# First feed-forward layer of a diffusion backbone: 14 of 22 hidden tiles as seven half-size products, in three segments with a written order

## The chip, the cores and the metric

One core of one Trainium2 chip runs the whole program. The metric is device time in microseconds (us). The engines are TensorE (matrix products; PE in the rows), VectorE (DVE), ScalarE (ACT), GpSimd (POOL) and SyncE (SP, which here only issues loads).

## The reference

Two layers over 512 latent tokens of width 1024. Layer 0 mixes tokens by latent attention with 256 context tokens and by a Fourier transform, layer 1 by two kinds of convolution. Each layer ends with the same channel mixer, a SwiGLU feed-forward of hidden width 2816 behind a modulated norm:

```python
sh1, sc1, g1, sh2, sc2, g2 = ada_mod(c, ada_w[i], ada_b[i])
...
x = x + g1 * mix
x = x + g2 * swiglu(modulate(rms_norm(x, norm2_g[i]), sh2, sc2), ffn_w1[i], ffn_w3[i], ffn_w2[i])
...
def swiglu(h, w1, w3, w2):
    return (jax.nn.silu(h @ w1) * (h @ w3)) @ w2
```

`ada_mod` turns the conditioning vector into six modulation vectors for each layer, 48 columns of 128 values.

## The kernel before

Everything is kept transposed: channels on the 128 partitions, the 512 tokens along the free axis. Each fp32 operand is split into a high part (rounded to fp32r) and a low part (the rest), and each product is three matmuls: high x high, high x low, low x high (`mm3`, L115). A weight unit (128 x 1024) is loaded by SP into a `wraw` buffer (three), its high part is cast on ScalarE and its low part is subtracted on VectorE (`split`, L95); five pairs `whi`/`wlo` hold the results.

**The plain form (layer 0, `ffn`, L996).** The hidden width is 22 tiles of 128, f = 0 to 21. For each, `proj` (L962) multiplies the norm's output by a w1 unit and a w3 unit: 8 steps over the channels x 3 matmuls x 512 tokens, twice, 48 matmuls. The first five units are done in two halves of the tokens, since the norm of the second half of the tokens is made meanwhile. Three of these five (the "head units", `HU`) lie in the large slots 14, 13 and 8. `done` puts Silu on the w1 result (ScalarE), multiplies it by the w3 result (VectorE, L1008) and splits the product into high and low. All 22 stay resident, then each of the 8 output tiles takes 22 x 3 matmuls of w2, and `residual` (L271) adds the result to `X`. The last output tile is done in two halves of 256 tokens, so that the statistics (`s1`) and the norm (`s2`, `s3`) of the next layer can start between.

**The block form (layer 1, `ffn_blocks`, L1046).** Here the first NPL = 3 tiles are plain and each further one is a 2 x 2 block product: rows are w1 and w3, inner halves are the channels 0 to 511 and 512 to 1023, columns are the tokens 0 to 255 and 256 to 511. Seven products of half size replace eight (Strassen's method in Winograd's form): 7 x 4 channel steps x 3 = 84 matmuls of 256 tokens (`prod`, L1188). It needs sums of the operands:
- of the norm's output, once: `forms` (L1084), four additions or subtractions of 128 x 1024 and four splits, from full copies of the norm's output that `Norm` then writes as well;
- of the weights, per tile: `load_sums` (L1113) has SP load one quarter twice into a tile and POOL add two other quarters by an accumulating transfer (L1120), then `prep_block` (L1122) makes two more sums on VectorE and splits them all. `load_raw` (L1107) loads the three quarters that are used as they are.

`block_window` (L1198) writes one tile's seven products together with the preparation of the next tile (`prep`) and the epilogue of the tile before (`tail`). The hidden tiles come in three segments of 8, 7 and 7 (`SEGS`); behind each, its part of the output product is added to `X`, so that only one segment's results need be kept.

**What sets the order.** In general the framework's scheduler orders the instructions of each engine by its own estimates and may hoist loads far ahead. From the end of `proj` in `ffn_blocks` the order is the written one (`manual_schedule`, L1262).

**Modulation columns.** Each column is a load of 128 x 1024 (512 KB) into one of two `ada` buffers and one VectorE reduction (L154), for some columns a ScalarE pass on 128 values. 56 columns, those that the end of layer 0 and layer 1 need, wait in a list `bg`; `pump(2)` (L178) runs two behind each hidden tile and output tile of layer 0.

Of the kernel before, what the change touches and what calls it, by code (L numbers as in the profile page):

```python
# [9 lines left out]
F32 = mybir.dt.float32  # L10
# [7 lines left out]
P = 128  # L18
# [15 lines left out]
FH = (5, 14)  # L34
# [27 lines left out]
def tile_dit(  # L62
# [100 lines left out]

    def ada_jobs(l, key, base, n, pin=True):
        m = const.tile([P, n], F32, name=f"m_{l}_{key}")
        mods[l, key] = m
        return [lambda j=j: ada_tile(m[:, j:j + 1], l * 48 + base + j, ada[l * 48 + base + j], scb, pin=pin)
                for j in range(n)]
# [9 lines left out]
    def pump(n):  # L178
        for _ in range(min(n, len(bg))):
            bg.pop(0)()  # L180

# [743 lines left out]
    n2_0 = Norm("n2_0", mods[0, "s2"])  # L925
# [6 lines left out]
    def ffn_srcs(l):  # L932
        return [w[l, f] for f in range(NPL if l in BLK else FF) for w in (w1, w3)]

# [61 lines left out]
    def ffn(l, nrm, head, sq_next=None, make_next=None):  # L996
        gt = {}
        held = {}

        def done(i, p):  # L1000
            f = i // 2
            if i % 2 == 0:
                s = t2k()
                A.activation(s, p, AF.Silu)
                held[f] = s
                return
            g = t2k()
            V.tensor_mul(g, p, held.pop(f))  # L1008
            if f in (4, 5):
                gt[f] = slot(("6a", "6b")[f % 2], [P, 2, S], F32R)  # L1010
            elif f % 2 == 0:
                d = slot(4 + f // 2, [P, 2, 2, S], F32R)
                gt[f], gt[f + 1] = d[:, 0], d[:, 1]
            split(gt[f][:, 0, :], gt[f][:, 1, :], g)
            pump(2)

        proj(ffn_srcs(l), nrm, done, NF, head=head)
        g2 = mods[l, "g2"]
        for mt in range(KT):
            chunks = [unit(w2[l, mt, :, a:a + n, :], n * P) for a, n in W2CHUNKS]  # L1020
            p = ps()
            nxt = None
            if mt == KT - 1 and make_next is not None:
                pump(len(bg))
                nxt = make_next()
            for hf, (a, b) in enumerate(((0, S),) if mt < KT - 1 else HALF):
                for ci, ((wh, wl), (k0, n)) in enumerate(zip(chunks, W2CHUNKS)):
# [528 lines left out]
```

## Time and profile before

| what | value |
|---|---|
| median of 3 runs | 1190.65 us (1190.1 to 1190.69) |
| profiled execution | 1190.21 us, span of the instructions 1188.3 us |
| TensorE / VectorE / ScalarE / POOL busy | 99% / 67% / 40% / 11% of the span |
| mean granted TensorE clock | 0.998 |
| feed-forward of layer 0 | about 297 to 662 us after the span's start |
| feed-forward of layer 1 | about 834 to 1185 us |
| read from memory | 174 MB |

Times in rows are us from the span's start. A row of the timeline gives start, duration, engine, line, operation, tiles written and read, and in brackets how long the engine had been idle before it and what ended that. Matmul durations overlap: the distance from one start to the next is what a matmul costs.

### The profile page before, as it was taken

How to read it: one execution, taken by the hardware profiler on the slowest of the kernel's cores; microseconds unless marked ns; L12 is line 12 of the kernel's file. 1: busy time of each engine (PE TensorE's matmuls, PEld its weight loads, DVE VectorE, ACT ScalarE, POOL GpSimd, SP SyncE). 2: the span in 40 equal slices, each digit the busy share in tenths (PEclk: the TensorE clock that was granted, in tenths of full speed). 3: DMA queues.
4: the chain of work that ended last, by engine and by line, in shares of the span. 5: the costliest groups of instructions: out<-in, count | busy, mean ns of one | idle time of the engine just before them, and what ended most of it. 6: DMA issues, size and time to landing. Idle time of an engine off the chain costs nothing.

```text
span 1188.3 us, 16786 instructions
## 1 busy us (share of the span) xinstructions
PE 1174.4 (99%) x6627; PEld 993.1 (84%) x6627; DVE 802.1 (67%) x1302; ACT 478.8 (40%) x787; POOL 127.6 (11%) x110
## 2 busy tenths in 40 slices
PE   8999999999999999999999999999999999999998
PEld 6777856669988888888888988888999899989997
DVE  7979876756665655554443699976887468757852
ACT  5545455544432323232222564334654235424530
POOL 1012300000000000000002496200000000000000
PEclk9999999999999999999999999999999999999999
DMA  9872033374266556655555133222168247816432
GB/s 340 300 286 109 1 106 93 120 248 144 67 216 209 181 189 200 197 182 188 167 162 168 54 106 107 72 89 90 49 181 221 91 109 185 219 54 162 107 110 86
DMA packets 52226, 177.24 MB, mean 149 GB/s; under 512 B 5682, under 2 KB 6578, under 8 KB 51891
## 3 DMA queue, kind: packets, MB, share of 16 engines
q1 hardware_dynamic: 49410, 166.21, 42.4%
q0 software_dynamic: 2736, 9.96, 4.9%
q8 instruction: 52, 0.85, 0.3%
q14 instruction: 28, 0.22, 0.1%
HBM read 174.05 MB, written 2.10 MB: 148 GB/s over the span
## 4 chain that ended last, share of the span: by engine, by line
PE 94%; DVE 3%; DMA 2%; ACT 1%; issue 0%; POOL 0%; ACTq 0%; DVEq 0%; SPq 0%
PE ps L116 21%; PE ps L117 21%; PE ps L118 21%; PE ps L1193 16%; PE ps L866 2%; PE ps L708 1%; PE ps L581 1%; PE ps L851 1%; PE ps L852 1%; PE ps L853 1%; PE ps L871 1%; DVE t L211 1%; DMA s<-in_w 1%; PE ps L822 1%; PE ps L197 1%; PE ps L293 1%
## 5 line engine op out<-in xcount | busy, mean ns | idle before, releaser
L116 PE MATMUL ps<-s,whi 128*128 128x512 f32 (+1 forms) x1067 | 394.9, 370 | 1.2 <-DVE x L272 1.2
L117 PE MATMUL ps<-s,whi 128*128 128x512 f32 (+1 forms) x1067 | 391.2, 367 | 2.1 <-DVE s L217 2.1
L118 PE MATMUL ps<-s,wlo 128*128 128x512 f32 (+1 forms) x1067 | 390.8, 366 | 0.2 <-DVE wlo L97 0.2
L96 ACT CAST whi<-wraw 128x1024 fp32r<-128x1024 f32 (+2 forms) x127 | 129.7, 1024 | 281.0 <-PE ps L117 138.5
L116 PEld LDWEIGHTS ps<-s,whi 128*128 128x128 f32 x1067 | 201.8, 189 | 36.1 <-DVE x L272 1.6
L117 PEld LDWEIGHTS ps<-s,whi 128*128 128x128 f32 x1067 | 201.8, 189 | 35.4 <-DVE s L217 2.3
L118 PEld LDWEIGHTS ps<-s,wlo 128*128 128x128 f32 x1067 | 201.8, 189 | 34.4 <-DVE wlo L97 0.7
L97 DVE TENSOR_TENSOR wlo<-wraw,whi 128x1024 fp32r<-128x1024 f32 (+2 forms) x107 | 127.1, 1188 | 79.8 <-ACT whi L96 76.3
L1193 PE MATMUL ps<-s,whi 128*128 128x256 f32 x912 | 165.2, 283 | 0.1
L1193 PEld LDWEIGHTS ps<-s,whi 128*128 128x128 f32 x912 | 142.4, 192 | 0.6 <-DVE t L1217 0.3
L1193 PE MATMUL ps<-s,wlo 128*128 128x256 f32 x456 | 129.0, 283 | 0.0
L272 DVE SCALAR_TENSOR_TENSOR x<-ps,m_g,x 128x512 f32<-128x512 f32 (+1 forms) x67 | 43.9, 662 | 105.9 <-PE ps L118 105.9
L154 DVE CUSTOM_DVE_ANT_0 ada<-ada,scb,vec 128x1024 f32<-128x1024 f32 x80 | 100.2, 1279 | 0.5 <-DMA ada<-in_ada 0.5
L1193 PEld LDWEIGHTS ps<-s,wlo 128*128 128x128 f32 x456 | 87.5, 192 | 0.0
L1120 POOL DMA_DIRECT2D s<-in_w x19 | 16.8, 884 | 585.9 <-DMA s<-in_w 443.7
L1008 DVE TENSOR_TENSOR t<-ps,t 128x512 f32<-128x512 f32 x22 | 15.2, 692 | 71.3 <-PE ps L118 71.3
L96 ACT CAST whi<-s 128x1024 fp32r<-128x1024 f32 x38 | 39.7, 1047 | 54.0 <-PE ps L1193 28.1
L1369 DVE SCALAR_TENSOR_TENSOR ps<-s,vec,ps 128x512 f32<-128x512 f32 x78 | 55.8, 751 | 1.4 <-ACT ps L1366 0.9
L97 POOL TENSOR_TENSOR wlo<-wraw,whi 128x1024 fp32r<-128x1024 f32 x20 | 48.8, 2444 | 30.9 <-ACT whi L96 27.0
L117 PE MATMUL ps<-s,s 128*128 128x256 f32 (+1 forms) x160 | 50.2, 315 | 0.0
L118 PE MATMUL ps<-s,s 128*128 128x256 f32 (+1 forms) x160 | 50.1, 314 | 0.0
L116 PE MATMUL ps<-s,s 128*128 128x256 f32 (+1 forms) x160 | 48.3, 317 | 0.2 <-ACT s L216 0.2
(278 smaller groups left out, 1662.2 us busy)
## 6 DMA issues: line engine op xcount, KB each, us to landing
ada<-in_ada SPq DMA_DIRECT2D x82, 512.0 KB, 4.4
wraw<-in_w SPq DMA_DIRECT2D x74, 512.0 KB, 3.6
s<-in_w SPq DMA_DIRECT2D x19, 768.0 KB, 5.7
wraw<-in_w_in SPq DMA_DIRECT2D x20, 512.0 KB, 3.3
s<-in_w SPq DMA_DIRECT2D x38, 256.0 KB, 4.0
s<-in_w POOLq DMA_DIRECT2D x19, 512.0 KB, 5.5
s<-in_ada SPq DMA_DIRECT2D x16, 512.0 KB, 7.1
wraw<-in_w_out SPq DMA_DIRECT2D x16, 512.0 KB, 3.4
```

What stands on the lines that cost most here:

```text
L96: A.copy(hi, src)
L97: (eng or V).tensor_sub(lo, src, f32(hi))
L116: T.matmul(o, wh, ah, start=start, stop=False)
L117: T.matmul(o, wh, al, start=False, stop=False)
L118: T.matmul(o, wl, ah, start=False, stop=stop)
L154: i = V.tensor_tensor_reduce(raw, raw, scv, 1.0, vc("ada_b", idx), ALU.mult, ALU.add, accum_out=dst)
L272: V.scalar_tensor_tensor(X[m][:, a:b], psum, gcol, X[m][:, a:b], ALU.mult, ALU.add)
L866: T.matmul(p[64 * x:64 * x + 64, :], vh[t][:, 2 * j + x, :], ost["p", 2 * j + x, tp][:, s * S:(s + 1) * S], start=(t == 0), stop=(t == 5))
L1008: V.tensor_mul(g, p, held.pop(f))
L1120: G.dma_start(s13, w[:, :D], accum_op=ALU.add)
L1193: T.matmul(o, w, b, start=start and kk == 0 and i == 0, stop=kk == 3 and i == 2, skip_group_check=True)
L1369: V.scalar_tensor_tensor(dst, cp[:, w:w + S], vec[:, o + w:o + w + 1], src, ALU.mult, ALU.add)
```

## The change

Layer 0's feed-forward also runs through `ffn_blocks`, which is made to take plain and block tiles in one sequence; `ffn` is deleted. Tiles 0 to 2 stay in `proj`. Of the other 19, fourteen are blocks (`BLK[0]`) and 5, 10, 13, 17 and 20 are plain (`plain_window`: the 48 matmuls with the same places for `prep` and `tail`). Every plain tile has block tiles as neighbours. The norm before layer 0's feed-forward writes full copies into slots 5 and 7. The sums of weights lie in the two halves of slot 8 in layer 0 and are loaded two blocks ahead (`SB`), not three. The output product has three segments here too, in written order; in the last segment the last three output tiles (`TS`) are left to the scheduler, first their left halves, then their right halves, with statistics and norm of layer 1 between. The modulation columns have fixed places: 4 behind tiles 0 and 1, then two in a window that does not lead from a block to a block of the same segment (13 of 19 windows), then two behind each of the first two output tiles of a segment and one behind each of the others. Each reduction is followed on SP by the load of the column two further on, into the buffer that the reduction frees.

```diff
-FH = (5, 14)
...
-W2CHUNKS = ((0, 8), (8, 8), (16, 6))
 SEGS = ((0, 8), (8, 7), (15, 7))
 NPL = 3
+NA = 2
 UB = 5
-BLK = {1: tuple(range(NPL, FF))}
+BLK = {0: (3, 4, 6, 7, 8, 9, 11, 12, 14, 15, 16, 18, 19, 21), 1: tuple(range(NPL, FF))}
...
+        def load(self):
+            self.raw = units.tile([P, D], F32, tag="ada", bufs=AB, name=nm("ada"))
+            nc.sync.dma_start(self.raw, ada[self.idx])
+        def reduce(self):
+            V.tensor_tensor_reduce(self.raw, self.raw, scb, 1.0, vc("ada_b", self.idx), ALU.mult, ALU.add, accum_out=self.dst)
...
+    def pump_ahead(n):
+        for _ in range(min(n, len(bg))):
+            while gains:
+                gains.pop(0)()
+            job = bg.pop(0)
+            job.reduce()
+            gains.append(job.gain)
+            if len(bg) >= AB:
+                bg[AB - 1].load()
...
-    n2_0 = Norm("n2_0", mods[0, "s2"])
+    n2_0 = Norm("n2_0", mods[0, "s2"], (5, 7))
...
-    def ffn(l, nrm, head, sq_next=None, make_next=None):
...
+            if l == 0:
+                if "s8" not in st:
+                    st["s8"] = slot(8, [P, 2, D])
+                return st["s8"][:, i % 2, :]
...
+            if f < NPL - 1:
+                pump(2)
...
+        SB = 3 if l else 2
...
+        def prep_tile(f):
+            if f in blk:
+                return prep_block(f)
+            wf[f] = []
+            return prep_two(wf[f], (w1[l, f], w3[l, f]), D)
...
+            pump_ahead(na - na // 2)
...
+        def plain_window(f, tail, prep, after, na):
+            hh, hl = nrm.h
+            pss = [ps(), ps()]
+            s, g = t2k(), t2k()
+            def mms(i):
+                wh, wl = wf[f][i]
+                for k in range(KT):
+                    c = slice(k * P, (k + 1) * P)
+                    mm3(pss[i], wh[:, c], wl[:, c], hh(k), hl(k), k == 0, k == KT - 1)
+            tail[0]()
+            prep[1]()
+            tail[1]()
+            prep[2]()
+            tail[2]()
+            mms(0)
+            prep[3]()
+            prep[4]()
+            A.activation(s, pss[0], AF.Silu)
+            pump_ahead(na - na // 2)
+            prep[5]()
+            mms(1)
+            prep[6]()
+            pump_ahead(na // 2)
+            after()
...
+        for job in bg[:AB]:
+            job.load()
...
+            for f in range(max(a, NPL), a + n):
+                if f in blk:
+                    load_sums(blk.index(f) + SB)
+                    load_raw(blk.index(f) + 2)
+                prep = nxt_prep or prep_at(f + 1)
+                if nxt_prep is None:
+                    prep[0]()
                 nxt_prep = None
                 after = nothing
-                if f + 2 < a + n:
-                    nxt_prep = prep_block(f + 2)
+                if f + 2 <= a + n:
+                    nxt_prep = prep_at(f + 2)
                     after = nxt_prep[0]
-                elif f + 2 == a + n:
-                    wload, wprep = two_units(wu, [w2src(0), w2src(1)], n * P)
-                    after = wload
-                tail = block_window(f, tail, prep, after)
+                na = 0 if f in blk and f + 1 in blk and f + 1 < a + n else NA
+                tail = (block_window if f in blk else plain_window)(f, tail, prep, after, na)
...
+            full = KT - TS if last and make_next is not None else KT
+            for mt in range(full):
+                w2_ahead(mt)
                 if not last and mt == KT - 3:
...
+                pump_ahead(2 if mt < 2 else 1)
...
+        nxt = make_next()
+        for mt in range(full, KT):
+            w2_ahead(mt)
+        pss = {mt: ps() for mt in range(full, KT)}
+        for mt in range(full, KT):
+            down(mt, 0, HS, pss[mt])
+        for i, mt in enumerate(range(full, KT)):
+            down(mt, HS, S, pss[mt])
+            if i < 2:
+                (nxt.s1, nxt.s2)[i](0)
+        nxt.s3(0)
+        return nxt
...
-    n1_1 = ffn(0, n2_0, head0, "n1_1",
+    n1_1 = ffn_blocks(0, n2_0, head0, "n1_1",
```

## Rows read from the trace of the kernel before

**Rows 1.** The page, busy time, share of the span and instructions of each engine.
```profile
PE 1174.4 (99%) x6627; PEld 993.1 (84%) x6627; DVE 802.1 (67%) x1302; ACT 478.8 (40%) x787; POOL 127.6 (11%) x110
```
**Rows 2.** Timeline of VectorE, layer 0: the product of the two halves of a tile.
```profile
324.21 0.69 DVE L1008 TENSOR_TENSOR t<-ps,t 128x512 f32<-128x512 f32 x1 [1.26 <-PE ps L118]
...
376.08 0.69 DVE L1008 TENSOR_TENSOR t<-ps,t 128x512 f32<-128x512 f32 x1 [3.19 <-PE ps L118]
...
506.64 0.69 DVE L1008 TENSOR_TENSOR t<-ps,t 128x512 f32<-128x512 f32 x1 [3.19 <-PE ps L118]
```
**Rows 3.** Timeline of VectorE, layer 1: the first subtraction of a block window.
```profile
988.05 0.42 DVE L1217 TENSOR_TENSOR t<-t,ps 128x256 f32<-128x256 f32 x1
...
1018.29 0.42 DVE L1217 TENSOR_TENSOR t<-t,ps 128x256 f32<-128x256 f32 x1
```
**Rows 4.** Windows: stretch, length, busy us of each engine, granted clock, DMA share, GB/s.
```profile
665.30:668.70 3.40, 3.40 (x18) 3.40 (x17) 3.40 (x5) 1.22 (x4) 2.66 (x1) 0.50 0.30 114
668.70:672.00 3.30, 3.30 (x27) 3.03 (x26) 2.59 (x8) 1.18 (x4) 0.70 (x1) 1.00 0.55 159
800.00:845.00 45.00, 44.87 (x310) 41.48 (x310) 32.04 (x63) 20.73 (x43) 1.67 (x2) 1.00 0.19 60
965.00:1036.00 71.00, 71.00 (x591) 70.91 (x590) 57.17 (x92) 33.15 (x57) 5.21 (x6) 1.00 0.70 180
```
**Rows 5.** Timeline of TensorE, layer 0: third head unit's end, tile 3's first matmul.
```profile
320.94 0.28 PE L118 MATMUL ps<-s,s 128*128 128x256 f32 x1
...
332.29 0.39 PE L116 MATMUL ps<-s,whi 128*128 128x512 f32 x1
```
**Rows 6.** Timeline, layer 1, second block's sums: SP, POOL, first reader on VectorE.
```profile
858.97 1.78 SPq L1119 DMA_DIRECT2D s<-in_w  x2
865.05 0.93 POOL L1120 DMA_DIRECT2D s<-in_w  x1 [23.26 <-DVE s L1140]
870.36 0.69 DVE L1137 TENSOR_TENSOR s<-s,s 128x512 f32<-128x512 f32 x1 [1.54 <-DMA s<-in_w]
```
**Rows 7.** Layer 1's first sums: SP, POOL, and the landing times of line L1120.
```profile
633.60 0.81 SPq L1119 DMA_DIRECT2D s<-in_w  x2
638.36 1.06 POOL L1120 DMA_DIRECT2D s<-in_w  x1 [333.54 <-DMA s<-in_w]
DMA to landing us min/median/max: 5.2/5.5/8.2
```
**Rows 8.** Timeline of VectorE, layer 1: preparation of the first block.
```profile
862.91 0.69 DVE L1137 TENSOR_TENSOR s<-s,s 128x512 f32<-128x512 f32 x1 [0.72 <-DMA s<-in_w]
...
866.46 2.36 DVE L97 TENSOR_TENSOR wlo<-s,whi 128x1024 fp32r<-128x1024 f32 x2
```
**Rows 9.** Timeline of TensorE, VectorE and POOL between the two layers.
```profile
653.17 0.39 PE L116 MATMUL ps<-s,whi 128*128 128x256 f32 x1 [0.58 <-DVE x L272]
664.37 0.39 PE L117 MATMUL ps<-s,whi 128*128 128x256 f32 x1 [2.07 <-DVE s L217]
660.13 3.79 DVE L211 SCALAR_TENSOR_TENSOR t<-x,m_s,rb 128x256 f32<-128x256 f32 x4 [4.02 <-ACT rb L205]
661.13 2.50 POOL L97 TENSOR_TENSOR wlo<-wraw,whi 128x1024 fp32r<-128x1024 f32 x1 [0.17 <-ACT whi L96]
```
**Rows 10.** Groups by form, VectorE, 318 to 540 us: the reduction of a modulation column.
```profile
L154 DVE CUSTOM_DVE_ANT_0 ada<-ada,scb,vec 128x1024 f32<-128x1024 f32 x42 | 52.2, 1280 | 0.0
```
**Rows 11.** The page's DMA issues: KB each, median us from issue to landing.
```profile
ada<-in_ada SPq DMA_DIRECT2D x82, 512.0 KB, 4.4
```
**Rows 12.** Timeline of VectorE: residual adds in layer 0, and in layer 1's first segment.
```profile
569.33 0.75 DVE L272 SCALAR_TENSOR_TENSOR x<-ps,m_g,x 128x512 f32<-128x512 f32 x1 [2.04 <-PE ps L118]
584.41 0.75 DVE L272 SCALAR_TENSOR_TENSOR x<-ps,m_g,x 128x512 f32<-128x512 f32 x1 [2.04 <-PE ps L118]
...
931.64 0.75 DVE L272 SCALAR_TENSOR_TENSOR x<-ps,m_g,x 128x512 f32<-128x512 f32 x1 [3.68 <-PE ps L118]
937.21 0.75 DVE L272 SCALAR_TENSOR_TENSOR x<-ps,m_g,x 128x512 f32<-128x512 f32 x1 [3.68 <-PE ps L118]
```

More of the change, by code (lines that the diff above doesn't have):

```diff
@@ L932, in ffn_srcs @@
     def ffn_srcs(l):
-        return [w[l, f] for f in range(NPL if l in BLK else FF) for w in (w1, w3)]
+        return [w[l, f] for f in range(NPL) for w in (w1, w3)]
     def head_units(l):
@@ L994, in proj @@
             done(i, p)
-    def ffn(l, nrm, head, sq_next=None, make_next=None):
[L997 to L1027, printed above, removed]
-                    for kk in range(n):
-                        f = k0 + kk
-                        c = slice(kk * P, (kk + 1) * P)
-                        mm3(p[:, a:b], wh[:, c], wl[:, c], gt[f][:, 0, a:b], gt[f][:, 1, a:b], f == 0, f == FF - 1)
-                        if nxt is not None and hf == 1 and f in FH:
-                            (nxt.s1, nxt.s2)[FH.index(f)](0)
-                residual(mt, p[:, a:b], g2[:, mt:mt + 1], a, b, sq_next)
-                if sq_next is None:
-                    nc.sync.dma_start(out[mt, :, a:b], X[mt][:, a:b])
-            pump(2)
-        if nxt is not None:
-            nxt.s3(0)
-        return nxt
     TSL = ((9, 10, 11, 12), (11, 12, 5, 7))
@@ L1193, in prod, with block_window @@
                     T.matmul(o, w, b, start=start and kk == 0 and i == 0, stop=kk == 3 and i == 2, skip_group_check=True)
-        def nothing():
-            pass
-        def block_window(f, tail, prep, after):
+        def block_window(f, tail, prep, after, na):
             w = wf.pop(f)
@@ L1253, in mid @@
             forms()
-            for i in range(3):
+            for i in range(SB):
                 load_sums(i)
@@ L1264, in ffn_blocks @@
         tail = [nothing] * 3
-        ready = {blk[0]: True}
+        for job in bg[:AB]:
+            job.load()
+        nxt = None
         for a, n in SEGS:
             last = a + n == FF
-            first = max(a, NPL)
             wu = []
@@ L1300, in down, with w2_ahead @@
                     mm3(p[:, c0:c1], wh[:, c], wl[:, c], gt[a + kk][:, 0, c0:c1], gt[a + kk][:, 1, c0:c1], kk == 0, kk == n - 1)
-                residual(mt, p[:, c0:c1], g2[:, mt:mt + 1], c0, c1, None)
-                if last:
+                residual(mt, p[:, c0:c1], g2[:, mt:mt + 1], c0, c1, sq_next if last else None)
+                if last and sq_next is None:
                     nc.sync.dma_start(out[mt, :, c0:c1], X[mt][:, c0:c1])
-            for x in tail:
-                x()
-            tail = [nothing] * 3
-            for mt in range(KT):
+            def w2_ahead(mt):
                 if mt + 3 < KT:
@@ L1314, in ffn_blocks @@
                     wu.append(u)
+            for x in tail:
+                x()
+            tail = [nothing] * 3
+            full = KT - TS if last and make_next is not None else KT
+            for mt in range(full):
+                w2_ahead(mt)
                 if not last and mt == KT - 3:
```

66 lines of the change are left out of this document (39 added, 27 removed).

## Prediction

> **What bounds the kernel now.** I read the page's engine totals first: TensorE is busy 99% of the span [rows 1]. Busy time alone does not prove a bound, so I read the cadence next. In the first layer's feed-forward, the evacuation of one tile follows that of the tile before by exactly 10.88 us, twelve times in a row [rows 2]: 48 matmuls of 512 columns, 226.7 ns each. In the second layer, which already has the block form, the same point of a block window recurs every 10.08 us [rows 3]: 84 matmuls of 256 columns, 120.0 ns each. Both cadences are free of gaps, so TensorE's instruction stream sets the end in both stages. VectorE is the next: in seven block windows (71 us) it is busy 57.17 us, 8.17 us each, and the DMA engines 70% [rows 4].
>
> **What the change removes.** 14 of 22 tiles go from 48 x 226.7 ns to 84 x 120.0 ns: 14 x (10.88 - 10.08) = **11.2 us less** on the path [rows 2, 3]. Both periods are rows of this kernel with these shapes, so nothing is extrapolated but the layer. From them, 512 and 256 columns differ by 106.7 ns, so each matmul carries a fixed 13.3 ns, and a block has 36 more of them: that fixed part is why 7/8 of the columns gives 7% and not 12.5%.
> The Trainium skill (TensorE: Matmul & The Clock Gate, "Back-to-back issue gap") puts that fixed part at 2.5 ns. By it a block would save 48 x 215.8 - 84 x 109.2 ns = 1.19 us, 16.6 us in all, an estimate from that page; the rows above differ, and the sum goes by the rows.
>
> **The first block: the step I expect to cost most.** The block needs sums of weights, made by two loads from SP and an accumulating transfer from POOL. In layer 0 both sum tiles lie in slot 8, which until then holds the third head unit. Its last matmul starts at 320.94, and the next tile's matmuls start at 332.29, where the first block window will start [rows 5]. In that window the first product needs only loaded weights; the second, at 332.29 + 12 x 0.12 = 333.73, needs the sums. Chain: issue about 321.2. In layer 1 a sum tile's loads issued at 858.97, POOL's instruction at 865.05 and the first reader at 870.36, 11.4 us [rows 6]: landed 332.6. Another pair, alone before, took 633.6 to 638.36 and at most 8.2 us to land, 13.0 us [rows 7]: 334.2. Then two adds, a cast and a subtraction. At the same place in layer 1 the first add starts at 862.91, and the subtractions of the pair start at 866.46, two in 2.36 us, so the first ends at 867.6: 4.7 us [rows 8], or 3.4 us if nothing of another step lies between. Ready between 336.0 and 338.9: TensorE stands **2.3 to 5.2 us; I take 3.5**, nearer the layer-1 chain, since the place is the same. Behind the waiting VectorE instruction stand the first block's further preparation and the epilogue of tile 2, none needed earlier.
> Layer 1 doesn't show this stall, because its first sums had been fetched some 230 us ahead into other buffers [rows 7]; what it waited for was only a plain load.
>
> **The clock behind it.** Where TensorE now waits 2.07 us, between the layers [rows 9], the granted clock is 0.50 (1.2 GHz) in the 3.4 us after it, with 18 matmuls where the next 3.3 us have 27 [rows 4]. A stall of 3.5 us at the first block should bring the same: one such stretch at half speed costs 0 to 1.7 us; I take **1.5**.
>
> **The norm ahead of the layer** now writes full copies, one more ScalarE pass for each of 16 half tiles. Layer 1 enters its feed-forward by the same code, and there TensorE is busy 44.87 of 45 us [rows 4]: 0 to 0.5, I take **0.3**. The 8 VectorE passes of the operand sums and splits (`forms`) stand beside units 0 to 5, as they do in layer 1. Without that cover they would cost some 9.8 us (8 passes of 1.22, as in [rows 8]); that is a rival below.
>
> **Windows.** Fixed order takes the scheduler's freedom. Layer 1 keeps 10.08 us in fixed order, so block windows cost nothing by themselves; a plain window has 10.88 us for less work of its own. New is the modulation reduction of 1.28 us [rows 10]: none where a block prepares a block, otherwise two, so 26 in 13 of the 19 windows, 4 before and 26 in the output stages. A block window with all its work and two reductions would be 8.17 + 2.56 = 10.73, 0.65 over the window; but the eight block windows that have reductions prepare only two plain units: two subtractions, where a block takes three, two adds and a shorter subtraction; so they stay under 10.08. A plain window that prepares a block has a shorter epilogue than a block window and stays under that 10.73, of 10.88. Each reduction is followed on SP by the load of the next but one, which waits for it; behind it stand the block loads of the following window, which are needed two windows later, some 20 us against an 11.4 us chain [rows 6]. POOL carries only accumulating transfers here. The two weight units of a plain tile are loaded ahead of the last product of the second window before it and cast after the second product of the next, some 4.3 us later, against 4.4 us for a load of this size [rows 11]; where it is late, ScalarE waits, and behind it stand a Silu and casts that have half a window to spare. Bounds 0 to 4 us; I take **0.3**, since layer 1's windows show no gap.
>
> **The output product** goes from one pass of 66 matmuls per output tile to three of 24 and 21. Now 15.08 us for 66 (228.5 ns); in layer 1's segments 5.57 us for 24 (232 ns) [rows 12]. The same 465 matmuls at full width: at 226.7 to 232 ns, -0.9 to +1.6 us against now. The halves at the end are 126 matmuls where 132 stood. I take **0.3**. The 16 further residual adds lie on VectorE beside matmuls.
>
> **The way into layer 1.** Now TensorE waits 0.58 us (the second half of the last tile uses the bank that the residual is reading) and 2.07 us for the norm, whose four VectorE passes take 3.79 us while POOL splits a weight unit at 661.13 [rows 9]; the half clock follows. After the change three tiles' left halves come first, so the bank wait goes (-0.6). Statistics and norm still have 21 matmuls (2.5 us) between each two steps, and the POOL splits remain: the second wait stays. From -4.3 (both waits and the half clock gone) to +3 (one more POOL pass in the chain); I take **-0.6**.
>
> **Sum:** -11.2 + 3.5 + 1.5 + 0.3 + 0.3 + 0.3 - 0.6 = **-5.9 us**. The profiled execution took 1190.21 us (span 1188.3, 1.9 around it) and would take 1184.3; the median is 0.44 above it, so 1184.75, say **1184.7 us**. Differences within 0.2% (2.4 us) can't be told from no change here.
>
> **Rivals.**
> 1. *The entry is covered* (chance 0.15). The sums come earlier, or other work hides their preparation, and the half clock behind the stall goes with it. Against it: the slot is held until 320.94 [rows 5]. Time: -5.9 - 3.5 - 1.5 = -10.9, 1179.8 us.
> 2. *VectorE, not the transfer, makes the first block late* (0.15). The modulation reductions of tiles 0 and 1 keep their place ahead of `forms`; if these start only after tile 1's evacuation (324.21 now [rows 2], with 1.4 us of its own and 2.6 us of reductions), forms end near 338.0, and the sums' preparation, behind them, at about 341.5: 7.8 us instead of 3.5, so -1.6: 1189.1 us. For it: the reductions are pinned to program order, and layer 1 has none there. Against: the scheduler may still put forms, whose inputs are ready earlier, ahead of them.
> 3. *Slower: the reductions wait for their loads* (0.10). With two buffers, two loads must land in every window with reductions. If the accumulating transfers stretch a landing from 4.4 us [rows 11] beyond the window's 10.08, VectorE stands, and its order is fixed: from there each us over costs 13 us in 13 windows. At 11 us: +12, 1196.8 us. For it: block windows alone keep the DMA engines 70% busy [rows 4]. Against: an average landing would have to more than double.
> 4. *The fixed cost of a matmul vanishes in layer 0's blocks and plain tiles* (0.02): without 36 x 14 x 13.3 ns a further 6.7 us less, 1178.0 us; [rows 2, 3], from both layers, speak against it. By the gap that the Trainium skill states (TensorE: Matmul & The Clock Gate, "Back-to-back issue gap") it would be 5.4 us, 1179.3 us, an estimate.
>
> **How the numbers follow.** The forecast's case has 0.58, its own range 1181 to 1188. Faster by over 0.2% (below 1188.3): 0.58 + 0.15 + 0.02 + 0.02 of rival 2 = 0.77; within: 0.13; slower: 0.10. The range takes in rival 1, rival 2 and the bounds of entry, output stage and layer change, and leaves out rival 3: **1178.5 to 1190.8**.
>
> **What would show it.** In the profile after: the block's recurring point in layer 0 every 10.08 us (right) or more (rival 3, with a wait of VectorE for the modulation tile); before the first block a TensorE wait of 2.3 to 5.2 us that ends on the sums' preparation, with the accumulating transfer as VectorE's releaser (right) or with `forms` just ended (rival 2); a granted clock of 0.5 behind it; a TensorE wait near 2 us at the start of layer 1. The prediction is wrong if the first block starts without a wait, or if windows with reductions are longer than the others.

## The result, and the profile after

| kernel | median | runs, range | ratio to before, 95% interval |
|---|---|---|---|
| before | 1190.65 us | 1190.1 to 1191.41 | |
| after | 1201.65 us | 5 runs, 1197.13 to 1204.47 | 1.0089 [1.0063, 1.0115] |

The change makes the kernel 0.9% slower; forecast were 1184.7 us and a range of 1178.5 to 1190.8. The profiled execution of after took 1201.65 us (span 1199.8), 11.4 more than that of before. Of the five runs of e9_plain_first, in the table of the experiments, one took 4048.96 us, over three times as long as the others; its ratio leaves that run out, and the median of the other four is 1197.57 us.

The totals of after (busy us, share of the span, instructions) against [rows 1]: TensorE issues 501 instructions more and is busy 4.8 us less, VectorE 91 us more.

```profile
PE 1169.6 (97%) x7128; PEld 1011.1 (84%) x7128; DVE 892.7 (74%) x1470; ACT 517.4 (43%) x879; POOL 138.7 (12%) x124
```

So TensorE now waits. Its list of waits in after (engine, tile and line that waited, releaser: us in total, times, longest) has three large new entries. L1190 is the matmul of a block product, L1212 VectorE's first subtraction in a block window, L95 ScalarE's cast of weights, L238 the statistics between the layers, L318 VectorE's add of the squares into `acc`.

```profile
PE ps L1190 <- DVE t L1212: 5.5, 10, 2.2
PE ps L1190 <- ACT whi L95: 4.8, 1, 4.8
PE ps L238 <- DVE acc L318: 4.3, 2, 4.0
```

That is 14.6 us in 13 waits; in before none of the three is there. Twelve of them are in layer 0 or at its end, places 1 to 5; the thirteenth is in layer 1, place 6.

**1. The first block.** SP's two loads of the first sum, POOL's accumulating transfers, VectorE's add that reads the sum, and TensorE's second product, in after's timeline:

```profile
320.30 0.81 SPq L1116 DMA_DIRECT2D s<-in_w  x2
322.97 0.98 SPq L1116 DMA_DIRECT2D s<-in_w  x2
...
326.03 1.05 POOL L1117 DMA_DIRECT2D s<-in_w  x1 [22.60 <-PE ps L117]
329.44 0.87 POOL L1117 DMA_DIRECT2D s<-in_w  x1 [2.37 <-DMA s<-in_w]
...
334.66 0.69 DVE L1134 TENSOR_TENSOR s<-s,s 128x512 f32<-128x512 f32 x1 [5.52 <-DMA s<-in_w]
...
337.69 0.80 PE L1190 MATMUL ps<-s,whi 128*128 128x256 f32 x2 [4.77 <-ACT whi L95]
```

VectorE stands 5.52 us for the transfer; the matmul before started at 332.64, so 5.05 us less one matmul of 0.12, 4.93 us, are lost; a wait of 0.46 us for a low part follows. The row's 4.77 counts from a modelled end: each stop costs about 0.15 us more than its row says.

**2. The clock.** Windows of after (stretch, length, busy us of each engine, granted clock, DMA share, GB/s): three stretches at the lower of the two clock levels (1.2 GHz), each beside or behind a wait, where before has one [rows 4].

```profile
320.00:332.60 12.60, 12.60 (x86) 11.64 (x85) 8.62 (x13) 3.39 (x5) 1.92 (x2) 1.00 0.90 257
334.90:341.80 6.90, 3.65 (x15) 3.36 (x16) 5.75 (x8) 3.83 (x5) 0.00 (x0) 0.51 0.48 120
...
553.40:556.80 3.40, 3.19 (x15) 3.19 (x16) 2.65 (x4) 1.35 (x2) 0.00 (x0) 0.50 0.84 278
...
662.60:669.40 6.80, 5.45 (x25) 5.45 (x26) 1.64 (x5) 1.77 (x3) 3.18 (x2) 0.50 0.29 86
```

TensorE in the second of them:

```profile
554.41 0.63 PE L1190 MATMUL ps<-s,whi 128*128 128x256 f32 x2
...
555.05 0.63 PE L1190 MATMUL ps<-s,whi 128*128 128x256 f32 x2
```

Three matmuls of 256 columns take 0.64 us there, 0.213 each instead of 0.120. In the first stretch TensorE stands until 337.69, so only 15 matmuls run at the low clock, 1.4 us more; the second costs 1.4 as well, the third 2.4. Before's one stretch costs 1.5, and is gone.

**3. Windows with reductions.** A reduction (L174) stands ahead of the first subtraction on VectorE; TensorE's fourth product writes the bank that the subtraction reads.

```profile
351.85 1.28 DVE L174 CUSTOM_DVE_ANT_0 ada<-ada,scb,vec 128x1024 f32<-128x1024 f32 x1
353.05 0.42 DVE L1212 TENSOR_TENSOR t<-t,ps 128x256 f32<-128x256 f32 x1
353.52 0.50 PE L1190 MATMUL ps<-s,whi 128*128 128x256 f32 x2 [0.24 <-DVE t L1212]
```

With that a block window takes 10.57 us (tile 4, 348.81 to 359.37 on TensorE) to 10.70, not 10.08. Eight windows have it, 4.2 us in all.

**4. The output stages.** On SP a column's load (L171) waits until a reduction has freed its buffer, and the w2 load behind it (L111) waits with it; ScalarE's cast then waits for the weights, VectorE's subtraction, residuals and the next segment's first subtraction come late:

```profile
522.80 3.13 SPq L171 DMA_DIRECT2D ada<-in_ada  x2
526.04 0.37 SPq L111 DMA_DIRECT2D wraw<-in_w  x1
...
525.37 0.95 ACT L95 CAST whi<-wraw 128x896 fp32r<-128x896 f32 x1 [7.33 <-DMA wraw<-in_w]
530.85 0.94 ACT L95 CAST whi<-wraw 128x896 fp32r<-128x896 f32 x1 [4.25 <-DMA wraw<-in_w]
...
553.14 0.41 DVE L1212 TENSOR_TENSOR t<-t,ps 128x256 f32<-128x256 f32 x1
...
553.61 0.79 PE L1190 MATMUL ps<-s,whi 128*128 128x256 f32 x2 [2.16 <-DVE t L1212]
```

**5. Between the layers** the statistics wait 4.03 us for VectorE's add, where before has only the 0.58 us wait of [rows 9].

**6. Layer 1.** Its first block window waits 1.35 us from start to start, where before loses 0.26:

```profile
885.98 0.50 PE L1190 MATMUL ps<-s,whi 128*128 128x256 f32 x2 [1.19 <-DVE t L1212]
```

It is in every run of the changed code, 0.8 to 1.8 us. VectorE comes to that subtraction late, since the first block's add waits 1.84 us for its load, against 0.72 before [rows 8]; POOL's next transfer and the second block's add, ahead of the subtraction, pass that on. Why the load lands later is open. A further 0.5 us is lost at 796 us.

**Sum**, from the starts of TensorE's matmuls: -11.2 us for the blocks; +7.4 in the first block's window (17.47 us, 1.4 of it the clock); +4.2 in the eight windows with reductions; +3.8 in the third segment's first window (13.88 us, 1.4 of it the clock); +1.5 for weights in the output stages; +4.2 for the statistics and +2.4 for the clock behind them; +1.3 for the norm that follows; +1.6 in layer 1. Before's bank wait, its half clock and two short waits in layer 0's norm are gone, -3.1. Together +12.1; from layer 0's feed-forward on the two traces differ by 11.9, and ahead of it after is some 0.4 us faster.

### The profile page after: what moved, and what is told of

It reads as the page before. It is cut to its first block, busy times and chain, and to the rows that moved or that the text cites. A ratio compares the mean times of both kernels' runs of the same rounds, so it can differ in the third digit from the quotient of the medians.

```text
span 1199.8 us, 18094 instructions
## 1 busy us (share of the span) xinstructions
PE 1169.6 (97%) x7128; PEld 1011.1 (84%) x7128; DVE 892.7 (74%) x1470; ACT 517.4 (43%) x879; POOL 138.7 (12%) x124
## 3 DMA queue, kind: packets, MB, share of 16 engines
q0 software_dynamic: 4752, 17.30, 8.7%
## 4 chain that ended last, share of the span: by engine, by line
PE 82%; DVE 7%; DMA 6%; ACT 2%; issue 2%; SPq 0%; POOL 0%; ACTq 0%; DVEq 0%
PE ps L1190 25%; PE ps L115 15%; PE ps L116 15%; PE ps L117 15%; DMA wraw<-in_w 3%; PE ps L903 2%; DMA s<-in_w 2%; DVE ada L174 1%; PE ps L745 1%; PE ps L618 1%; PE ps L888 1%; ACT whi L95 1%; PE ps L889 1%; PE ps L890 1%; DVE wlo L96 1%
## 5 line engine op out<-in xcount | busy, mean ns | idle before, releaser
L1190 PE MATMUL ps<-s,whi 128*128 128x256 f32 x1584 | 291.3, 285 | 10.3 <-DVE t L1212 5.5
L115 PE MATMUL ps<-s,whi 128*128 128x512 f32 (+1 forms) x806 | 294.0, 365 | 2.6 <-ACT s L253 1.7
L117 PE MATMUL ps<-s,wlo 128*128 128x512 f32 (+1 forms) x806 | 290.1, 360 | 1.4 <-DVE wlo L96 1.4
L116 PE MATMUL ps<-s,whi 128*128 128x512 f32 (+1 forms) x806 | 290.4, 360 | 1.1 <-DVE s L254 0.9
L1190 PEld LDWEIGHTS ps<-s,whi 128*128 128x128 f32 x1584 | 249.9, 194 | 13.5 <-DVE t L1212 7.5
L1190 PE MATMUL ps<-s,wlo 128*128 128x256 f32 x792 | 225.4, 285 | 0.5 <-DVE wlo L96 0.5
L95 ACT CAST whi<-wraw 128x1024 fp32r<-128x1024 f32 (+1 forms) x105 | 105.8, 1014 | 170.4 <-DMA wraw<-in_w 98.0
L1190 PEld LDWEIGHTS ps<-s,wlo 128*128 128x128 f32 x792 | 153.2, 193 | 0.8 <-DVE wlo L96 0.8
L96 DVE TENSOR_TENSOR wlo<-wraw,whi 128x1024 fp32r<-128x1024 f32 (+1 forms) x85 | 99.5, 1171 | 39.8 <-ACT whi L95 39.2
L95 ACT CAST whi<-s 128x1024 fp32r<-128x1024 f32 x66 | 68.6, 1046 | 85.4 <-PE ps L1190 33.8
L96 DVE TENSOR_TENSOR wlo<-s,whi 128x1024 fp32r<-128x1024 f32 x66 | 80.1, 1221 | 7.8 <-ACT whi L95 5.2
L174 DVE CUSTOM_DVE_ANT_0 ada<-ada,scb,vec 128x1024 f32<-128x1024 f32 x52 | 66.3, 1280 | 6.2 <-DMA ada<-in_ada 6.2
L1190 PE MATMUL ps<-s,u 128*128 128x256 f32 x396 | 52.9, 283 | 0.0
L96 POOL TENSOR_TENSOR wlo<-wraw,whi 128x1024 fp32r<-128x1024 f32 x20 | 48.9, 2450 | 31.2 <-ACT whi L95 27.5
L116 PE MATMUL ps<-s,s 128*128 128x256 f32 (+1 forms) x160 | 50.3, 314 | 0.0
L117 PE MATMUL ps<-s,s 128*128 128x256 f32 (+1 forms) x160 | 50.2, 314 | 0.0
```

Of the source, the lines that this page charges most:

```text
L95: A.copy(hi, src)
L96: (eng or V).tensor_sub(lo, src, f32(hi))
L115: T.matmul(o, wh, ah, start=start, stop=False)
L116: T.matmul(o, wh, al, start=False, stop=False)
L117: T.matmul(o, wl, ah, start=False, stop=stop)
L174: V.tensor_tensor_reduce(self.raw, self.raw, scb, 1.0, vc("ada_b", self.idx), ALU.mult, ALU.add, accum_out=self.dst)
```

## The experiments

Each changes after unless said otherwise. In the diffs, lines are shortened to what differs. Before was run again beside each batch (medians 1190.21 to 1190.58 us). The intervals reach 1 to 2.5 us to either side, so a gain of 3 us against after says little by itself, and the traces have to say where it lies.

| label | edit | median us | ratio to before, interval |
|---|---|---|---|
| e1_no_mod | no reductions from tile 3 on, nor their loads | 1184.67 | 0.9947 [0.9930, 0.9965] |
| e8_no_mod_out | none in the output stages, nor their loads | 1188.24 | 0.9985 [0.9975, 0.9995] |
| e3_pump_after | reduction behind the subtraction | 1194.5 | 1.0032 [1.0019, 1.0046] |
| e5_pool_loads | column loads from POOL | 1194.93 | 1.0036 [1.0023, 1.0049] |
| e2_sum_early | first sums in slot 6b | 1198.44 | 1.0060 [1.0039, 1.0080] |
| e4_head_dve | layer 1's first splits on VectorE | 1198.28 | 1.0062 [1.0046, 1.0077] |
| e6_three | e2 + e3 + e5 | 1187.57 | 0.9976 [0.9967, 0.9985] |
| e7_four | e6 + e4 | 1187.31 | 0.9975 [0.9963, 0.9986] |
| e9_plain_first | tile 3 plain, 5 a block | 1198.13 | 1.0057 [1.0041, 1.0073] |
| e10_last_clear | last output stage free | 1203.38 | 1.0103 [1.0085, 1.0121] |
| e11_five | e6 + e10 | 1181.89 | 0.9927 [0.9912, 0.9942] |
| e12_plain_all | e3 + e5 + e9 + e10 | 1180.24 | 0.9913 [0.9898, 0.9928] |
| e13_dummy | e11 + six reductions without a buffer | 1184.46 | 0.9949 [0.9934, 0.9964] |
| e14_pool_clear | e5 + e10 | 1188.65 | 0.9982 [0.9973, 0.9992] |
| e15_final | e12 + e4 | 1178.89 | 0.9902 [0.9885, 0.9918] |

### What do the blocks give, and what do the reductions cost?

```diff
-            job.reduce(); gains.append(job.gain)
-            if len(bg) >= AB:
-                bg[AB - 1].load()
```


> The change with its 52 modulation reductions from tile 3 of layer 0 onward left out, and their loads (the columns hold a constant instead). Theory A, the places of the reductions are the cause: each load of a column stands on SP behind a reduction, so weight loads behind it are late, and VectorE's written order passes that on. Then the waits of about 0.4 us in the block windows (3.2 us in all), the 4.3 us at the first block of the third segment and the 6 us more between the layers all go, and only the 7.9 us at the first block stay: 1201.65 - 13.5 = about 1188 us. Rival B, the layer change is late by POOL's splits and a cast that waits for layer 1's weights: only the first two go, about 1194 us. Rival C, neither depends on the reductions: 1201 us.

1184.67 us, 17.0 under after. The last subtraction of two neighbouring block windows of layer 0, VectorE in e1:

```profile
378.29 0.42 DVE L1228 TENSOR_TENSOR t<-t,ps 128x256 f32<-128x256 f32 x1 [0.88 <-PE ps L1188]
388.37 0.42 DVE L1228 TENSOR_TENSOR t<-t,ps 128x256 f32<-128x256 f32 x1 [1.02 <-PE ps L1188]
```

10.08 us, as in layer 1 [rows 3]. The blocks give what was forecast. Without the reductions and their loads the loss in layer 0 is gone, but for the first block's window and the norm between the layers. That it hangs on their places, and not on their number, is for e12 to show, which has them all. Leaving out only those of the output stages:

```diff
-                pump_ahead(2 if mt < 2 else 1)
```


> The change with the reductions of the three output stages left out (26 columns hold a constant instead), those of the windows kept. It parts the 17 us that the reductions cost in all: if the output stages' places cost most (third segment's first block 4.3, layer change 6), about 1190 us, and the waits of 0.4 us in the windows stay. If the windows' places cost most, about 1197 us.

1188.24: 13.4 of the 17.0 us come from the output stages and what follows them (the waits at 553 us and of the statistics are gone), 3.6 from the windows (4.2 by the windows' lengths).

### Is it VectorE's order, or SP's?

```diff
-            pump_ahead(na - na // 2)
             prod(m6, w["s2"], st["T2"])
             V.tensor_sub(q[:, :HS], q[:, HS:], m6)
+            pump_ahead(na - na // 2)
```


> The change with the first reduction of a block window written behind the first subtraction (which reads the second product's result from the bank that the fourth product writes) instead of ahead of it. Theory: the waits of about 0.4 to 0.5 us in the block windows with reductions are that subtraction being 1.28 us late: they go, 8 x 0.4 = 3.2 us less, about 1198.5 us, windows of 10.08 us. Rival: VectorE is late by itself, and the wait only moves to the next reader: 1201 us, windows of 10.5 us.

7.2 us less, where 3.2 were forecast. The short waits in the windows are gone and the windows are 10.08 us long, 4.2 us less. Another 2.4 us are in the first block's window, ahead of which nothing was changed; the rest is not accounted for. Of the wait for the first subtraction 3.5 us in two places are left: 2.3 at the third segment, as in place 4, and 1.2 in layer 1, as in place 6.

```diff
-            nc.sync.dma_start(self.raw, ada[self.idx])
+            G.dma_start(self.raw, ada[self.idx])
```


> The change with all its reductions, but the loads of their columns issued by POOL instead of SP; nothing else moves. Theory A1, the order on SP is what hurts: a column's load waits on SP for a reduction, and the weight loads behind it for the load. With SP free the casts no longer wait for weights, VectorE is on time at the ends of the output stages: the 4.3 us at the third segment's first block go and most of what the layer change has more than before (6 us); the 0.4 us waits in the windows stay: 1201.65 - 4 to -9 = 1193 to 1198 us. Rival A2, it is VectorE's work itself (1.28 us for each reduction, in a place where it is full): no gain, 1201 us, the casts still late or the subtractions late without waiting for a cast. Rival A3: POOL's own issue work beside VectorE costs more: slower than 1202 us.

6.7 us less. The wait at 553 us is gone with the half clock behind it (3.8 us together), and so are most of the waits for weights in the output stages. The short ones in the eight windows stay, and so does that of the statistics (5.3 us): there SP's column loads are not the cause by themselves. The edit also moves these loads to another DMA queue (q0 carries 44.57 MB in e5, 17.30 in after); the runs don't part that from the order on SP.
The Trainium skill (SBUF — State Buffer, "SBUF: two separate sides") warns of loads issued by GpSimd, since a VectorE operation in a two-port mode can keep it from writing their descriptors. Here the column loads land in a median of 4.8 us from POOL against 3.8 from SP in after, and the kernel is faster all the same; whether VectorE delayed any of them is not shown.

### The first block

```diff
+                if i == 0:
+                    return slot("6b", [P, D])
                 if "s8" not in st:
```


> The change with the first block's sum tile in slot 6b, which is free long before, instead of slot 8. Theory: the 4.93 us wait of TensorE at the first block and the half clock behind it (some 2 to 3 us) come from slot 8 being held by the third head unit: both go, 1201.65 - 7 to 7.9 = about 1194 us. Rival: VectorE's queue (operand sums and four reductions ahead of the preparation) would have been late as well: a wait of 2 us or more stays before the second product, 1198 us or more.

3.2 us less. The first block's sums now come early, but TensorE still stands 1.63 and 0.71 us there. In e6, which has the same edit, one sees why: VectorE has the second block's add, which waits 2.56 us for its transfer, ahead of the first block's last subtractions. Moving the whole block instead:

```diff
-BLK = {0: (3, 4, 6, ...
+BLK = {0: (4, 5, 6, ...
-            run_prep(prep_block(blk[0]))
+            run_prep(prep_tile(NPL))
```


> The changed kernel with tile 3 plain and tile 5 a block instead (still 14 blocks): the block's sums get one more window, 10.9 us, to arrive. Theory (transfer into slot 8 is what the first block waits for): the 4.9 us stall at the first pair's second product and the half clock behind it are gone, first pair 21 us instead of 28.0, about 7 us less than the changed kernel: 1193 to 1197. Rival (VectorE's backlog from the operand sums and the pinned reductions, whatever tile comes first): the stall moves to the first plain window or into the next block, total within 2 us of 1201.65.

1198.13 (1197.57 without the one long run), 3.5 to 4.1 us less and not 7. The wait and the half clock at the first block are gone (TensorE is busy 26.00 of 26 us from 331). But a wait of 1.5 us comes in the second block's window, where the third block's add waits 2.42 us for its transfer; and one window fewer takes reductions, so that the last output stage has eight, not six. In the last two output stages TensorE waits 3.7 us for low parts and 2.0 us for casts of weights, against 1.4 and under 0.6 in after. The price of the first block has to be read where the layer change is mended (below).

### Between the layers

```diff
-        head += [unit(s, D, lo_eng) for s in srcs[len(head):first]]
+        head += [unit(s, D) for s in srcs[len(head):first]]
```


> The change with the low parts of the first three weight units of layer 1's projection made on VectorE, not on POOL. Theory: POOL's subtractions stretch VectorE's additions into the sum of squares from 0.43 us to 2.4 and 3.05 us, and these hold the statistics between the layers: the wait of 4.03 us there falls by 3 us or more, and the half clock behind it with it, about 1197 us. Rival: VectorE comes late out of the output stage, or ScalarE's squares stand behind a cast that waits for a load: the wait stays, and VectorE has 3.7 us more to do: 1201 to 1204 us.

3.4 us less, but that doesn't speak for the edit. In its trace the first block's window takes 14.50 us, 3.0 less than in after, and up to there the programs are the same. The statistics wait 3.36 us instead of 4.03, not 3 us less. The three edits together:

> Three edits at once: the first sums early (slot 6b), the first reduction of a block window behind the first subtraction, the columns' loads on POOL. If the causes are separate, their gains add: entry 3 to 7, windows 3 to 7, output stages 4 to 9: about 1185 us, below the kernel before (1190.3). If one of them only hides another (VectorE being late everywhere), they don't add: 1192 us or more.

and with this one:

> The three edits, and the low parts of the first three weight units of layer 1's projection on VectorE instead of POOL. Theory: what is left between the layers (a wait of about 2 us for the norm and a half clock, as in the kernel before) comes from POOL's subtractions beside VectorE's passes: 2 to 4 us less than with the three edits. Rival: with VectorE on time the 3.7 us more work there cost as much as they save: no difference.

1187.57 and 1187.31: the four alone sum to 20.5 us, together they give 14.3. In e7 the statistics wait 2.2 us, in e6 5.1, so POOL's splits have a part in that wait; the time is the same within the noise. In e6 the wait of the statistics is 5.1 us, and its chain can be read, since nothing else disturbs it (L1118 the sums' loads on SP, L1119 POOL's accumulation, L105 layer 1's weight loads, L96 splits):

```profile
628.89 1.28 DVE L174 CUSTOM_DVE_ANT_0 ada<-ada,scb,vec 128x1024 f32<-128x1024 f32 x1
633.38 1.28 DVE L174 CUSTOM_DVE_ANT_0 ada<-ada,scb,vec 128x1024 f32<-128x1024 f32 x1
...
630.21 1.30 SPq L1118 DMA_DIRECT2D s<-in_w  x2
634.70 0.80 SPq L1118 DMA_DIRECT2D s<-in_w  x2
637.99 21.70 SPq L105 DMA_DIRECT2D wraw<-in_w_in  x6
...
643.69 0.88 POOL L1119 DMA_DIRECT2D s<-in_w  x1 [7.43 <-PE ps L117]
644.26 5.00 POOL L96 TENSOR_TENSOR wlo<-wraw,whi 128x1024 fp32r<-128x1024 f32 x2
...
644.43 1.05 ACT L95 CAST whi<-wraw 128x1024 fp32r<-128x1024 f32 x1 [3.37 <-DMA wraw<-in_w_in]
...
645.83 3.72 DVE L318 TENSOR_TENSOR acc<-acc,t 128x256 f32<-128x256 f32 x1 [3.91 <-ACT t L317]
...
650.97 1.01 PE L238 MATMUL ps<-ones,acc 128*128 128x2 f32 x4 [5.09 <-DVE acc L318]
```

The last two reductions end at 630.2 and 634.7, and just then SP issues the loads of layer 1's first sums, whose tiles share the `ada` buffers. These pairs of 256 KB loads and layer 1's weights now travel at the same time: the unit issued at 637.99 is cast at 644.43, and ScalarE's square for the statistics is behind that cast. POOL's splits stand behind the accumulating transfer, fall on VectorE's add and stretch it from 0.43 to 3.72 us. VectorE itself is idle for 3.91 us.

If that is so, a last output stage without reductions must clear it:

```diff
-                na = 0 if f in blk and f + 1 in blk and f + 1 < a + n else NA
+                na = 1 if f in blk and f + 1 in blk and f + 1 < a + n else NA
```


> The changed kernel with one reduction in each of the six windows that lead from a block to a block of the same segment, so that the last output stage before layer 1 has none left (all 56 are still done). Theory (the last reductions hold the two column buffers, into which layer 1's first sums are loaded; on SP the first weight loads of layer 1 stand behind these; ScalarE's cast waits for them with the squares behind it): the 4.0 us wait of the statistics is gone, layer change 20 us as in the kernel before instead of 25.9, the six windows stay within 0.3 us, 1194 to 1197 us. Rival (POOL's splits beside VectorE stretch the adds of the statistics, whatever the reductions do): a wait of 2 to 5 us stays there, 1199 to 1202.

(The one reduction stands at the later of the two places of a block window.) The wait of the statistics is gone, as the theory has it, but the time is 1203.38, above both ranges: the windows with one reduction wait instead. In one of them, e10:

```profile
445.94 1.28 DVE L174 CUSTOM_DVE_ANT_0 ada<-ada,scb,vec 128x1024 f32<-128x1024 f32 x1
...
447.25 0.33 SPq L171 DMA_DIRECT2D ada<-in_ada  x1
447.67 0.92 SPq L111 DMA_DIRECT2D wraw<-in_w  x2
...
455.06 1.05 ACT L95 CAST whi<-wraw 128x1024 fp32r<-128x1024 f32 x1 [4.64 <-DMA wraw<-in_w]
...
457.75 0.98 PE L1190 MATMUL ps<-s,u 128*128 128x256 f32 x6 [2.11 <-DVE t L1217]
```

SP issues the weights 0.4 us behind the column's load, and that 0.03 us behind the reduction. Then taking the column loads off SP must cure these windows:

> The changed kernel with two edits: the last output stage free of reductions (alone 1203.38) and the columns' loads issued by POOL (alone 1194.93). Theory (on SP a load that waits for a reduction holds up the weight loads behind it, in the windows too): the waits of 1.2 to 2.3 us in the windows with one reduction are gone, those of 0.4 us stay, the first block's wait stays, the statistics' wait is gone: 1185 to 1189. Rival (the denser reductions on VectorE make the windows late): waits of over 1 us stay in these windows, 1192 or more.

1188.65. TensorE's waits for block products in e14: in layer 0 none over 0.4 us but the first block's; these short ones stay, as expected.

```profile
PE ps L1190 <- ACT whi L95: 3.6, 1, 3.6
PE ps L1190 <- DVE t L1212: 3.5, 9, 1.2
```

(The 1.2 of the second row is in layer 1, at 873.20, as in place 6.) So the column loads' place on SP made e10's waits, not the load on VectorE. All edits of e6 and this one:

> The three edits together (first sums in slot 6b, first reduction of a block window behind the first subtraction, columns' loads from POOL), which took 1187.57, and the last output stage free of reductions. Theory: the statistics' wait of 5.3 us goes, and with it a half clock of 6.8 us: 1179 to 1183 us, under both kernels. Rival (denser reductions make the windows wait): 1185 to 1189.

1181.89, under both kernels. Last, is it the buffers, or VectorE's time, that the last reductions cost?

```diff
                 pump_ahead(2 if mt < 2 else 1)
+                if last and make_next is not None and mt < 4:
+                    for _ in range(2 if mt < 2 else 1):
+                        V.tensor_tensor_reduce(st["junk"], scb, scb, ...)
```


> The five-edit kernel (three edits and the last output stage free, 1181.89 us) with six operations of the same kind and size as a reduction put back on VectorE at the places that the last output stage's reductions had; they read the resident conditioning tile and write a spare slot, so they hold no column buffer and need no load; their result is not used. Theory (the column buffers, held to the end, push layer 1's first sums and the accumulating transfers into the layer change): no wait of the statistics over 1 us, total within 2 us of 1181.89. Rival (VectorE's own lateness, some 1.5 us at the last residuals, starts the chain): the wait of 2 to 5 us is back, 1185 to 1189.

2.6 us more than e11, though the intervals overlap, and the wait of the statistics is back in part:

```profile
647.71 0.61 PE L238 MATMUL ps<-ones,acc 128*128 128x2 f32 x4 [1.52 <-DVE acc L318]
```

Neither theory alone: of the 5.1 us that this wait had in e6, 1.5 come back with VectorE's time; by difference, the other 3.6 belong to the buffers and what waits for them. Which of these, the accumulating transfers ahead of POOL's splits or the loads beside layer 1's weights, has the larger part was not tried.

### A version that beats both

> Tile 3 plain and tile 5 a block, first reduction of a block window behind the first subtraction, columns' loads from POOL, last output stage free of reductions (sums all in slot 8). Theory: no wait at the first block, none at the statistics, half clock only at the norm: the kernel before less 11.2 us for the blocks plus 1 to 3 us of small waits, 1179 to 1182 us. Rival (the fixed order costs elsewhere as much as it saves there): 1185 to 1189.

1180.24 us, 10.4 under before and 21.4 under after, with all the work of after done. VectorE is busy 891.2 us in it, as in after (892.7). Two rows of TensorE's waits in e12, the longest behind the first load of the program:

```profile
PE ps L115 <- ACT s L253: 1.8, 1, 1.8
...
PE ps L1190 <- DVE t L1211: 1.1, 1, 1.1
```

The first is the norm between the layers, the second is in layer 1, as in place 6. All blocks of layer 0 but one (10.21 us) take 10.08 us, and in its trace no half clock is left there. Against e11, which has e12's other edits and the sums in slot 6b, the plain first tile is worth 1.7 us; the intervals overlap. (In e11's trace the first block window is still 3.6 us too long.)

> The fastest kernel so far (1180.24 us: tile 3 plain, reduction behind the subtraction, loads from POOL, last output stage free) with the low parts of layer 1's first three units subtracted on VectorE instead of POOL. If POOL's splits stretch the norm's VectorE passes: the wait of 1.95 us before the second half of the norm falls to about 1.3 and the half clock with it at most, 1178 to 1180. Rival (the three passes of 1.2 us on VectorE stand in the norm's own chain): same or up to 1 us slower.

1178.89; the interval overlaps that of e12. The wait of the norm is 1.79 us in both, so POOL's splits of these units are not its cause. But in e15 POOL still splits a later unit, just ahead of the norm's passes (L248; L242 copies the factor `rb` that they need):

```profile
650.77 2.39 POOL L96 TENSOR_TENSOR wlo<-wraw,whi 128x1024 fp32r<-128x1024 f32 x1 [2.64 <-ACT whi L95]
650.91 0.35 ACT L242 COPY rb<-ps 128x256 f32<-128x256 f32 x1
651.04 2.40 DVE L318 TENSOR_TENSOR acc<-acc,t 128x256 f32<-128x256 f32 x1 [0.84 <-ACT t L317]
653.36 1.26 DVE L248 SCALAR_TENSOR_TENSOR t<-x,m_s,rb 128x256 f32<-128x256 f32 x3
```

`rb` is there at 651.26, and VectorE's add stands ahead of the passes for 2.40 us, where one alone takes 0.43. So this split is the likely cause of the wait: without it the passes could start some 1.9 us earlier, an estimate. In before a split lies beside the passes themselves, four in 3.79 us [rows 9]. No run moved this unit, so it stays argued.

## Why the prediction was wrong, step by step

- **Blocks, -11.2: right.** 10.08 us in layer 0 as soon as nothing else disturbs (e1, and e12 with all the work). The fixed 13.3 ns per matmul hold.
- **First block, +3.5: right in kind.** It waits for the accumulating transfer, as said: 4.93 us in after, within the bounds. Up to there the programs of after, e3, e4, e8 and e10 are the same, yet the row's wait is 4.8, 2.2, 1.7, 3.6 and 3.6 us, and the chain (320.30 to 334.66 in after) takes 14.4, 11.8, 11.3, 13.2 and 13.2 us, where 11.4 to 13.0 were taken. The DMA engines are 90% busy there in after and 92% in e3 and e4, so that share doesn't explain the difference; it stays open. A wait of 0.5 to 0.8 us for a low part, behind the first, was not in the sum. With it and the clock the window is 7.4 us over 10.08 in after, where 3.5 + 1.5 were taken.
- **The clock behind it, +1.5: right.** Half speed for 6.9 us, not 3.4, but TensorE stood for the first part of it: 15 matmuls, 1.4 us.
- **Norm with full copies, +0.3: no cost.** The first block window starts at 331.33, tile 3 before at 332.29 [rows 5].
- **Windows, +0.3: failed.** The step added up VectorE's time (8.17 + 2.56 us) and found it under the period. But TensorE doesn't wait for a sum: it waits for one subtraction, and the reduction is written ahead of that. The price is 4.2 us. e3 shows it: with the same work, two lines later, the windows are 10.08 us long.
- **The load behind a waiting load: failed.** The text said that a column's load waits for a reduction on SP and asked only whether block loads have slack (20 us). The plain units stand in the same queue with some 4.3 us; that slack was named, and its bound (0 to 4 us) kept out of the sum. The w2 units of the output stages, in the same queue, were not considered. With the column loads on POOL (e5) the 3.8 us at the third segment and most of the 1.5 us for weights go.
- **Output product, +0.3: right for the matmuls** (465 of them take 106.1 us, 105.4 at 226.7 ns), wrong for what stands behind: 3.8 us at the third segment with the clock (e5, e8: gone).
- **Way into layer 1, -0.6: failed.** The bank wait is gone, but 4.03 us for the statistics (4.2 from start to start), 2.4 for the clock and 1.3 for the norm came, beyond the bound of +3. The step looked at POOL's passes and the 21 matmuls between; it didn't follow the last reductions' buffers to layer 1's sums.
- **Layer 1: put at nothing.** Its feed-forward runs the code that the change rewrote; its first block window is 1.1 us longer, and 0.5 us go ahead of it (place 6).
- **Rival 3 had the sign but not the mechanism.** Its condition, columns landing in over 10 us, did not come (median 3.8 in after, 4.4 before [rows 11]), and VectorE waited for columns only 6.2 us in all. The wait runs the other way: the loads wait for the reductions, and the weights for the loads. Its "from there each us over costs 13" was the wrong place to price, too.

The range failed because the three steps that failed were bounded one by one, each with its own cover, though one list of 56 reductions and one queue run through all of them: they fail together, and the range had no case for that.

## What to carry to other kernels

When work that frees a buffer gets a fixed place, write down for every queue what is issued behind the load that refills it, and the slack of the tightest of these, not of the most frequent. When an operation is put on an engine with time to spare, ask which short instruction behind it a busier engine waits for; the sum of busy times doesn't answer that. A buffer pool shared by two stages couples them: the last user of the first sets when the second may load.

## What the hardware showed

- **VectorE's adds end when POOL's pass ends.** An add of two resident operands, 0.43 us alone, took 3.72 us in e6 (ends 649.55; POOL's splits end 649.26), and twice in after:

```profile
655.45 3.05 DVE L318 TENSOR_TENSOR acc<-acc,t 128x256 f32<-128x256 f32 x1
660.18 2.35 DVE L318 TENSOR_TENSOR acc<-acc,t 128x256 f32<-128x256 f32 x1 [1.68 <-ACT t L317]
...
655.47 2.74 POOL L96 TENSOR_TENSOR wlo<-wraw,whi 128x1024 fp32r<-128x1024 f32 x1
659.91 2.34 POOL L96 TENSOR_TENSOR wlo<-wraw,whi 128x1024 fp32r<-128x1024 f32 x1 [1.71 <-ACT whi L95]
```

  The adds end 0.29 and 0.28 us behind the splits. The Trainium skill (SBUF — State Buffer, "SBUF: two separate sides") says that VectorE with two SBUF inputs and a GpSimd operation that reads SBUF hold one port pair in turn, for a whole instruction each. The ends agree; in the first pair the add's row starts 0.02 us ahead of the split's, so the starts don't tell who came first.
- **The same wait is not always followed by a low clock.** After the 1.79 us wait of the norm (it ends at 655.97), e1 ran at 0.52 from 662.9 to 666.3; e12, with the same wait, at 1.00 throughout:

```profile
653.00:657.00 4.00, 3.63 (x28) 3.22 (x27) 4.00 (x7) 2.72 (x6) 2.47 (x1) 1.00 0.28 111
657.00:661.00 4.00, 3.24 (x25) 3.03 (x26) 3.66 (x10) 1.31 (x3) 0.46 (x2) 1.00 0.39 131
661.00:665.00 4.00, 3.99 (x34) 3.79 (x33) 2.36 (x6) 1.68 (x4) 0.43 (x1) 1.00 0.00 0
```

  That, and the first block's window, 14.50 to 17.47 us in programs that are the same up to there, are likely reasons why after's runs are 7 us apart and before's 1.3 (3.8 over 13 runs of a later batch). Neither was tried by itself.
